# Indexer queries gathered in long runs, sums of squares after one projection, and one broadcast per factor in a two-layer transformer kernel

## The chip, the cores and the metric

The kernel runs on one core of one Trainium2 chip, in one launch. The metric is the device time of the whole launch in microseconds (us); a time "before" is the median of several executions on the chip.

## The reference, cut to what matters

Two identical layers work on 512 tokens of width 1024. Each layer projects the tokens with one matrix, runs two kinds of attention on the pieces (eight heads of latent attention, eight heads of sparse attention), mixes them, and applies a mixture of 16 experts. What the change touches is this:

```python
proj = h @ w_in
qa, kva, kr, dq, dk, dv, iq, ik, iw = split(proj)      # iq: 8 heads x 32
# latent attention
q    = rms_norm(qa, q_norm_g) @ w_q_up                  # qa: 384 wide
c_kv = rms_norm(kva, kv_norm_g)                         # kva: 256 wide
v    = c_kv @ w_uv
# sparse attention: an indexer chooses 128 keys per token
rel   = relu(einsum('bthd,bsd->bths', iq, ik) * 32 ** -0.5)
score = einsum('bths,bth->bts', rel, iw * 8 ** -0.5)
sel   = top_k(where(key <= token, score, -inf), 128)
...
def rms_norm(x, g):
    return x * rsqrt(mean(x * x) + 1e-6) * g
```

## The kernel before, in words

The function `attention(l, ...)` builds one layer's attention. All 512 tokens lie along the free axis of a tile, and the projection is made in 13 column tiles of 128 (`proj(ct)`, L242 to L272). Each column tile is 24 matmuls of 128x128 by 128x512 (L271): the weights are split into a high and a low half (`split`, L163 and L164), and high by high, low by high and high by low are added. The high half is a cast on ScalarE (ACT, L163). The low half is a subtraction of 128x1024 elements (L164), on VectorE (DVE) or GpSimd (POOL); from the fourth column tile on it is on GpSimd. The column tiles come in this order: one small one, two with the indexer's queries (iq), the one with the sparse keys and values (dkv), two with kva, three with qa, four with dq.

**Indexer.** The queries of a column tile are written to memory (`iqd`, L301) and read back by four DMAs (L304), eight a layer, so that one head's 32 rows lie beside one another on 32 partitions. Then, for three blocks of query tokens (i = 1, 2, 3, with 256, 384 and 512 keys) and eight heads each, TensorE makes the scores (L347), ScalarE applies the relu (L352), and VectorE adds the weighted heads (L355 for the first head, L358 for the other seven). The top 128 follow in 16 rounds of a maximum and a replacement on VectorE (MAX, L365, and MATCH_REPLACE, L366), then a comparison (L368) and the distance mask (L372). These rounds are filler: they carry a lower priority, and the scheduler puts them where VectorE has nothing more urgent.

**Norms.** ScalarE squares kva (L336) and qa into `sqk`, `sqq` and `sq2`; GpSimd adds the two squares of kva (L381). TensorE sums over the partitions with matmuls against a column of ones (L418, 4 for kva and 12 for qa in a layer); VectorE divides by the width (`ms`, L422); GpSimd raises to the power -0.5 (`rmsy`, L185) and writes each factor onto a diagonal (`dg`, L427, one instruction of 512 columns for the kva factor and one for the qa factor). A matmul of a matrix of ones with the diagonal (L434) gives every partition the factor of each token: the broadcast. VectorE multiplies kva by it (`kvg`, L439), GpSimd makes the low half of the product (L164, `big<-kvg`), and the value products (L220, L221, L223) and the query products with their scaling (L530) come after.

**Order.** The kernel is built with a scheduler. It places each instruction on its engine's list by priority (the order in which the code is written, lowered for the filler) and by its own estimate of when the inputs are ready; `tc.issue_after(x)` adds the condition that an instruction stands behind x. Each engine then runs its list in order and waits where an input isn't there. So a change in one place can turn the list in another. Hardware queues: all loads and the iq transfers are issued from SyncE.

Of the kernel before, what the change touches and what calls it, by code (L numbers as in the profile page):

```python
# [17 lines left out]
L, T, D = 2, 512, 1024  # L18
NT = T // 128
# [76 lines left out]
def block_kernel(ctx, tc, xT0, x0, win, wqk, wuv, wo, gvec, lnp, rw, rb, wgu, wdn, consts, angles, stripd, rowsd, out):  # L96
    nc = tc.nc
# [19 lines left out]
    def C(name, a=0, b=None):  # L117
        o, w = _C[name]
        return cn[:, o + a:o + (w if b is None else b)]
# [33 lines left out]
    def ps(tag):  # L153
        return psp.tile([128, 512], F32, name=tag, bufs={"mm": 4, "tr": 2, "pv": 2}[tag])

    def bigt(dt=F32):
        return big.tile([128, 2048], dt, name="big")
# [55 lines left out]
    iqd = drm.tile([2, 2, 128, 384], F32, name="iqd")  # L213
# [17 lines left out]
    def attention(l, xh, xl, wraw, first, rest, x_dram):  # L231
# [5 lines left out]
                    load_win(l, i, wraw)  # L237
            return wraw[s]

        done = {}  # L240

        def proj(ct):  # L242
            if l and ct == 0:
# [23 lines left out]
        def project(p, w, ts, jj=(0, 1, 2), end=2):  # L267
            for j in jj:
                for k in range(8):
                    x = (xl if j == 2 else xh)[k // 4][:, k % 4, ts]  # L270
                    nc.tensor.matmul(p[:, ts], w[j == 1][:, k * 128:(k + 1) * 128], x, start=(j + k == 0),  # L271
                                     stop=(j == end and k == 7))  # L272

        ke, ko = x4p("ke")
        at = u4("at")
# [10 lines left out]
        p = proj(T_S)  # L286
# [8 lines left out]
        iq = [bigt(F32R)[:, :1536].rearrange("p (h t) -> p h t", h=4) for _ in range(2)]  # L295
        for i in range(2):
            p = proj(T_IQ + i)
            iqp = u4("iqp", F32R)
            split(iqp[:, :512], iqp[:, 512:], p)

            nc.sync.dma_start(iqd[i].rearrange("j p t -> p j t"),  # L301
                              iqp.bitcast(F32).rearrange("p (j t) -> p j t", j=2)[:, :, 128:])
            for j in range(4):
                nc.sync.dma_start(iq[i][32 * j:32 * (j + 1)].bitcast(F32),  # L304
                                  iqd[i][j // 2].rearrange("(h r) t -> r h t", h=4))
        p = proj(T_DKV)
        dkv, sq2 = u4p("dkv")
        nc.scalar.copy(dkv, p)
# [5 lines left out]
        p = ps("mm")  # L314
# [6 lines left out]
        p = transpose4(dkv, 0)  # L321
        nc.scalar.copy(dvt, p.rearrange("p (a b) -> p a b", a=NT)[:, :, 64:128])
        p = transpose4(S, 0)
# [7 lines left out]
        sqk = u4p("sqk")  # L331
# [7 lines left out]
        for i in range(1, NT):  # L339
# [3 lines left out]
            for h in range(8):  # L343
                if (i, h) in KVA_AT:
                    latents(KVA_AT.index((i, h)))
                p = ps("mm")
                nc.tensor.matmul(p[:, :n], iq[h // 4][:, h % 4, (i - 1) * 128:i * 128], ik4[:, :n],  # L347
                                 start=True, stop=True)
                if h % 4 == 0:
                    rel = bigt()  # L350
                r = rel[:, h % 4 * 512:(h % 4 + 1) * 512]
# [18 lines left out]
            for dd in DD[i]:  # L370
                w = dd.shape[1]
# [27 lines left out]

        dqs = [bigt(F32R).rearrange("p (a b) -> p a b", a=4) for _ in range(2)]  # L400
        vs = bigt().rearrange("p (a b) -> p a b", a=4)
        for i in range(4):
            p = proj(T_DQ + i)
            qh, ql = u4p("dq", F32R)
            nc.scalar.activation(qh, p, AF.Copy, scale=-0.125)
            nc.vector.scalar_tensor_tensor(ql, p, -0.125, qh.bitcast(F32), op0=OP.mult, op1=OP.subtract)
            for s in range(2):
                d = dqs[i // 2][:, i % 2 * 2 + s, :]
                for j, q in enumerate((qh, ql)):
                    b = 64 * (s ^ j)  # L410
                    copy_rows(d[b:b + 64], q[64 * s:64 * (s + 1)])
            if i == 1:

                p = ps("pv")
                for j, qq in enumerate((sqk[:1], sqq)):
                    for t in range(NT):
                        for q in qq:
                            nc.tensor.matmul(p[:, j * 4 + t:j * 4 + t + 1], q[:, t * 128:(t + 1) * 128],  # L418
                                             C("ones", 0, 1), start=(q is qq[0]), stop=(q is qq[-1]))
                ms = sm.tile([128, 8], F32, name="ms")  # L420
                for j, n in enumerate((256, 384)):
                    nc.vector.tensor_scalar(ms[:, 4 * j:4 * j + 4], p[:, 4 * j:4 * j + 4], 1.0 / n, 1e-6,  # L422
                                            op0=OP.mult, op1=OP.add)
                rs, _ = rsqrt(ms, 8, "rms")
                dgt = u4("dg")
                for j in range(2):
                    nc.gpsimd.tensor_tensor(dgt[:, j * 512:(j + 1) * 512].rearrange("p (t a) -> p t a", t=NT),  # L427
                                            ident[:, None, :].to_broadcast([128, NT, 128]),
                                            rs[:, 4 * j:4 * j + 4][:, :, None].to_broadcast([128, NT, 128]), op=OP.mult)
            if i == 2:  # L430
                bc = []
                for j in range(2):
                    p = ps("pv")
                    nc.tensor.matmul(p, C("ones"), dgt[:, j * 512:(j + 1) * 512], start=True, stop=True)  # L434
                    bc.append(p)
        ckt = bigt(F32R)
        ckv = [(ckt[:, 1024 * i:1024 * i + 512], ckt[:, 1024 * i + 512:1024 * (i + 1)]) for i in range(2)]
        for i in range(2):
# [998 lines left out]
def layouts(a):  # L1437
# [4 lines left out]
    qa, kva, kr, dq, dk, dv, iq, ik, iw = np.split(w, np.cumsum([384, 256, 32, 512, 64, 64, 256, 32]), axis=2)  # L1442
    sw = np.concatenate([kr[:, :, 16:], kr[:, :, :16]], axis=2)
    pad = np.zeros((L, D, 24), w.dtype)
    cols = np.concatenate([ik, iw, pad, kr, sw, iq, dk, dv, kva, qa, dq], axis=2)
    win = c(cols.reshape(L, 8, 128, N_COLT, 128).transpose(0, 2, 3, 1, 4)).reshape(L, 128, N_COLT * 1024)
    q = a["w_q_up"].reshape(L, 384, 8, 96)
# [46 lines left out]
```

## Time and profile before

| | |
|---|---|
| median of 3 runs | 1209.43 us (1207.76 to 1210.98) |
| the profiled execution's own time | 1213.77 us |
| its span in the profile | 1212.0 us |
| TensorE matmuls (PE) busy | 1150.3 us, 95% of the span |
| VectorE (DVE) busy | 1026.7 us, 85% |
| ScalarE (ACT) busy | 802.6 us, 66% |
| GpSimd (POOL) busy | 303.4 us, 25% |
| mean granted TensorE clock | 0.98 |

The profile is one execution. Its own time is 4.34 us above the median of the runs and 1.77 us above its span. Shares of busy time are means over very different stages: in the experts TensorE is nearly always busy, while in the attention stage, at 40 to 138 us in the first layer and about 640 to 740 us in the second, VectorE is the busy one. A timeline row gives start, duration, engine, line, operation, output<-inputs and shapes; a bracket gives the idle time before it and what ended it. A row "x2" holds two such instructions in a row.

### The profile page before, as it was taken

What the parts mean: (1) busy time and instruction counts of PE and PEld (TensorE: products, weight loads), DVE (VectorE), ACT (ScalarE), POOL (GpSimd) and SP (SyncE); (2) the same over time, 40 slices, a digit from 0 to 9 for tenths busy, and PEclk for the clock granted to TensorE, in tenths of its full rate; (3) what the DMA queues carried; (4) which work ended last, traced back from release to release, by engine and by line L of the source; (5) the groups of instructions that cost most, each with busy time, mean ns of one, the idle gap of its engine ahead of it and who ended that gap; (6) DMA issues with size and microseconds to landing.
All of it is one profiled execution on the core that took longest, in us unless ns stands there. A gap on an engine that the chain in (4) does not pass through costs nothing. (4 is left out here: it accounts for less than half of the span.)

```text
span 1212.0 us, 16822 instructions
## 1 busy us (share of the span) xinstructions
PE 1150.3 (95%) x5729; PEld 901.6 (74%) x5729; DVE 1026.7 (85%) x1857; ACT 802.6 (66%) x1264; POOL 303.4 (25%) x241
## 2 busy tenths in 40 slices
PE   9999899999999999999898998999999999999995
PEld 6686556778788888887686765567777888888783
DVE  4599977389999999988867999674899999999987
ACT  4533578335788888887544346683358888888872
POOL 2336332121211111200542453322211111111004
PEclk8999999999999999999898999999999999999998
DMA  7626104456999999988235270143669999999841
GB/s 253 200 67 218 51 12 141 161 208 252 391 392 396 388 384 369 383 317 299 84 137 143 70 253 1 51 141 144 234 269 379 400 390 387 394 373 368 304 170 69
DMA packets 56972, 292.20 MB, mean 241 GB/s; under 512 B 10064, under 2 KB 13904, under 8 KB 28465
## 3 DMA queue, kind: packets, MB, share of 16 engines
q1 hardware_dynamic: 47376, 270.48, 60.2%
q0 software_dynamic: 8064, 15.36, 3.5%
q10 hardware_dynamic: 1440, 5.24, 1.1%
q8 instruction: 46, 0.75, 0.2%
q14 instruction: 46, 0.37, 0.1%
HBM read 267.96 MB, written 31.98 MB: 247 GB/s over the span
## 5 line engine op out<-in xcount | busy, mean ns | idle before, releaser
L163 ACT CAST hl<-big 128x1024 fp32r<-128x1024 f32 x438 | 457.1, 1054 | 132.1 <-PE mm L635 46.2
L164 DVE TENSOR_TENSOR hl<-big,hl 128x1024 fp32r<-128x1024 f32 x403 | 483.5, 1226 | 49.7 <-ACT hl L163 42.9
L1056 PE MATMUL mm<-hl,xh 128*128 128x512 f32 x504 | 206.7, 410 | 0.0
L1057 PE MATMUL mm<-hl,xh 128*128 128x512 f32 x504 | 197.4, 392 | 0.0
L1078 PE MATMUL pv<-hl,hT 128*128 128x512 f32 x720 | 172.0, 394 | 0.8 <-DVE hl L164 0.8
L1078 PEld LDWEIGHTS pv<-hl,hT 128*128 128x128 f32 x720 | 136.4, 190 | 30.0 <-DVE hl L164 1.7
L271 PE MATMUL mm<-big,hl 128*128 128x512 f32 (+1 forms) x624 | 141.9, 387 | 1.9 <-ACT hl L163 1.0
L271 PEld LDWEIGHTS mm<-big,hl 128*128 128x128 f32 x624 | 114.3, 195 | 26.8 <-ACT hl L163 2.5
L1020 POOL DMA_INDIRECT xg<-xdr,ii x30 | 53.7, 1790 | 265.0 <-DVE ii L1034 238.9
L164 POOL TENSOR_TENSOR hl<-big,hl 128x1024 fp32r<-128x1024 f32 x35 | 85.9, 2458 | 134.1 <-ACT hl L163 118.8
L1056 PEld LDWEIGHTS mm<-hl,xh 128*128 128x128 f32 x504 | 94.8, 188 | 16.2 <-ACT hl L163 0.3
L1057 PEld LDWEIGHTS mm<-hl,xh 128*128 128x128 f32 x504 | 95.1, 189 | 15.7
L1056 PE MATMUL mm<-hl,xl 128*128 128x512 f32 x252 | 98.8, 392 | 0.0
L1057 PE MATMUL mm<-hl,xl 128*128 128x512 f32 x252 | 98.6, 391 | 0.0
L635 PE MATMUL mm<-hl,big 128*128 128x512 f32 x384 | 95.1, 401 | 0.0
L492 ACT ACTIVATE P<-P,mn 128x128 f32<-128x128 f32 (+3 forms) x128 | 71.9, 568 | 18.6 <-DVE mn L490 16.5
L635 PEld LDWEIGHTS mm<-hl,big 128*128 128x128 f32 x384 | 71.9, 191 | 14.1
L504 ACT COPY big<-tr 128x512 f32<-128x512 f32 (+3 forms) x128 | 49.7, 431 | 36.4 <-PE tr L502 35.5
L502 PE MATMUL tr<-cn,P 128*128 128x128 f32 x320 | 61.8, 293 | 9.8 <-DVE P L498 9.3
L502 PEld LDWEIGHTS tr<-cn,P 128*128 128x128 f32 x320 | 36.0, 141 | 42.8 <-ACT big L504 17.0
L1098 POOL DMA_INDIRECT ydr<-y,ii x26 | 28.2, 1085 | 151.4 <-ACT y L1094 114.1
L572 POOL TENSOR_TENSOR mh<-dd,cn 128x256 f32<-128x256 f32 (+2 forms) x64 | 44.6, 717 | 66.0 <-DVE mn L490 39.8
(279 smaller groups left out, 1861.1 us busy)
## 6 DMA issues: line engine op xcount, KB each, us to landing
big<-wgu SPq DMA_DIRECT2D x128, 1024.0 KB, 8.6
big<-wdn SPq DMA_DIRECT2D x64, 1024.0 KB, 8.2
big<-win SPq DMA_DIRECT2D x10, 1024.0 KB, 5.6
ydr<-zz SPq DMA_DIRECT2D x2, 4096.0 KB
big<-wo SPq DMA_DIRECT2D x8, 1024.0 KB, 14.0
big<-ydr SPq DMA_DIRECT2D x8, 1024.0 KB, 5.3
big<-wqk SPq DMA_DIRECT2D x4, 1024.0 KB, 4.8
big<-dq SPq DMA_DIRECT2D x32, 128.0 KB, 2.3
```

Source lines behind the costliest of these rows:

```text
L163: i = nc.scalar.copy(hi, src).ins
L164: last_lo[0] = (eng or nc.vector).tensor_sub(lo, src, hi.bitcast(F32)).ins
L271: nc.tensor.matmul(p[:, ts], w[j == 1][:, k * 128:(k + 1) * 128], x, start=(j + k == 0), stop=(j == end and k == 7))
L492: nc.scalar.activation(e, e, AF.Exp, bias=mn[:, i:i + 1], scale=-1.0, accum_out=su[:, i:i + 1])
L502: nc.tensor.transpose(p[:, (i - kb) * 128:(i - kb + 1) * 128], P[:, PO[i] + kb * 128:PO[i] + (kb + 1) * 128], ident)
L504: copies.append(nc.scalar.copy(pt[kb], p[:, :512 - 128 * kb]).ins)
L572: last_mask[0] = nc.gpsimd.tensor_tensor(m[:, c:c + w], dd, C("slope", h, h + 1).to_broadcast([128, w]), op=OP.mult)
L635: R["pe"] = nc.tensor.matmul(pp[t][i], x, w[:, i * 512:(i + 1) * 512], start=first, stop=last).ins
L1020: return nc.gpsimd.indirect_dma_start(out=st[e]["xg"], out_offset=None, in_=xdr[l], in_offset=bass.IndirectOffsetOnAxis(ap=st[e]["ii"][:, ...
L1056: nc.tensor.matmul(pg, x, w[:, :512], start=(k == 0 and x is a and w is wh), stop=last)
L1057: nc.tensor.matmul(pu, x, w[:, 512:], start=(k == 0 and x is a and w is wh), stop=last)
L1078: nc.tensor.matmul(py[i], x, w[:, i * 512:(i + 1) * 512], start=(k == 0 and x is a and w is wh), stop=last)
```

## The change

1. On the host, the columns of iq are put in the order (row, head) in place of (head, row), and the DMA of L304 reads 32 runs of 4 heads x 384 tokens instead of 32 times 4 runs of 384 tokens (6144 bytes in a piece where it was 1536). The number of DMAs and their bytes are the same.
2. The four sums for kva, so far free to run as soon as their input was there, are held behind the last matmul of the second dq projection with `issue_after`, together with the twelve for qa.
3. The two broadcasts, so far both behind the third dq projection in the code, are now written one behind the third (kva's) and one behind the fourth (qa's).

```diff
@@ proj, project @@
-        done = {}
+        done, last_mm = {}, [None]
...
-                    nc.tensor.matmul(p[:, ts], w[j == 1][:, k * 128:(k + 1) * 128], x, start=(j + k == 0),
-                                     stop=(j == end and k == 7))
+                    last_mm[0] = nc.tensor.matmul(p[:, ts], w[j == 1][:, k * 128:(k + 1) * 128], x,
+                                                  start=(j + k == 0), stop=(j == end and k == 7)).ins
@@ the queries' way back from memory @@
                 nc.sync.dma_start(iq[i][32 * j:32 * (j + 1)].bitcast(F32),
-                                  iqd[i][j // 2].rearrange("(h r) t -> r h t", h=4))
+                                  iqd[i][j // 2].rearrange("(r h) t -> r h t", h=4))
@@ dq projections, i in 0..3 @@
+        bc = []
...
             if i == 1:
                 p = ps("pv")
-                for j, qq in enumerate((sqk[:1], sqq)):
-                    for t in range(NT):
-                        for q in qq:
-                            nc.tensor.matmul(p[:, j * 4 + t:j * 4 + t + 1], q[:, t * 128:(t + 1) * 128],
-                                             C("ones", 0, 1), start=(q is qq[0]), stop=(q is qq[-1]))
+                with tc.issue_after(last_mm[0]):
+                    for j, qq in enumerate((sqk[:1], sqq)):
+                        for t in range(NT):
+                            for q in qq:
+                                nc.tensor.matmul(p[:, j * 4 + t:j * 4 + t + 1], q[:, t * 128:(t + 1) * 128],
+                                                 C("ones", 0, 1), start=(q is qq[0]), stop=(q is qq[-1]))
...
-            if i == 2:
-                bc = []
-                for j in range(2):
-                    p = ps("pv")
-                    nc.tensor.matmul(p, C("ones"), dgt[:, j * 512:(j + 1) * 512], start=True, stop=True)
-                    bc.append(p)
+            if i >= 2:
+                bc.append(ps("pv"))
+                nc.tensor.matmul(bc[-1], C("ones"), dgt[:, (i - 2) * 512:(i - 1) * 512], start=True, stop=True)
@@ host @@
+    iq = iq.reshape(L, D, 2, 4, 32).transpose(0, 1, 2, 4, 3).reshape(L, D, 256)
     cols = np.concatenate([ik, iw, pad, kr, sw, iq, dk, dv, kva, qa, dq], axis=2)
```

The scheduler turns these edits into new lists; both layers change alike. Line numbers of the changed kernel differ by one or two (L418 is L420, L422 is L424, L427 is L429, L439 is L438). On TensorE, from the sums to the value products (L220), the end of the list before is this:

```order
L418 MATMUL pv<-cn,dkv 128x1
L271 MATMUL mm<-big,hl 128x512 x24
L434 MATMUL pv<-dg,cn 128x512 x2
L271 MATMUL mm<-big,hl 128x512 x24
L220 MATMUL mm<-hl,big 128x512
```

and in the changed kernel:

```order
L420 MATMUL pv<-cn,dkv 128x1
L271 MATMUL mm<-big,hl 128x512 x30
L434 MATMUL pv<-dg,cn 128x512
L271 MATMUL mm<-big,hl 128x512 x18
L434 MATMUL pv<-dg,cn 128x512
L220 MATMUL mm<-hl,big 128x512
```

The first broadcast stands six matmuls into the fourth dq projection, the second at its end. The four kva sums, before behind the fifth of the third block's eight scores (L347), now stand right ahead of the twelve qa sums, after 120 matmuls of five projections.

GpSimd's list around the diagonals, before:

```order
L381 TENSOR_TENSOR sqk<-sqk 128x512
L164 TENSOR_TENSOR hl<-big,hl 128x1024 x4
L164 TENSOR_TENSOR hl<-wv,hl 128x1024
L185 TENSOR_TENSOR rmsy<-ms,mhalf 128x8
L427 TENSOR_TENSOR dg<-cn,rmsy 128x512 x2
L164 TENSOR_TENSOR hl<-big,hl 128x1024 x2
L164 TENSOR_TENSOR big<-kvg,big 128x512 x2
L448 MEMSET zz 128x1024
```

and in the changed kernel:

```order
L381 TENSOR_TENSOR sqk<-sqk 128x512
L164 TENSOR_TENSOR hl<-big,hl 128x1024 x4
L185 TENSOR_TENSOR rmsy<-ms,mhalf 128x8
L164 TENSOR_TENSOR hl<-wv,hl 128x1024
L164 TENSOR_TENSOR hl<-big,hl 128x1024
L429 TENSOR_TENSOR dg<-cn,rmsy 128x512 x2
L164 TENSOR_TENSOR hl<-big,hl 128x1024
L164 TENSOR_TENSOR big<-kvg,big 128x512 x2
```

Two low halves, of `wv` and of a dq weight, now stand between the power (`rmsy`) and the diagonals. VectorE's list around the kva product, as a difference (minus is before, plus is the change; the numbered tiles are the rounds' maxima):

```order
 L365 MAX m_520<-aw 128x8
-L406 SCALAR_TENSOR_TENSOR dq<-mm,dq 128x512
-L439 TENSOR_TENSOR kvg<-kvg,pv 128x512 x2
 L366 MATCH_REPLACE aw<-m_520,aw 128x384
+L407 SCALAR_TENSOR_TENSOR dq<-mm,dq 128x512
+L438 TENSOR_TENSOR kvg<-kvg,pv 128x512 x2
 L365 MAX m_523<-aw 128x8
```

The product stands one replacement later. Past this, the lists of the softmax stages of both layers also differ in many places, by a few instructions each.

## Rows read from the trace of the kernel before

**Rows 1.** Waits of VectorE, 40 to 138 us: output line <- releaser: us, times, longest

```profile
DVE aw L355 <- ACT big L352: 7.3, 1, 7.3
DVE big L164 <- ACT big L163: 1.4, 1, 1.4
```

**Rows 2.** Timeline of TensorE, second layer, indexer

```profile
640.73 0.73 PE L347 MATMUL mm<-ik,big 128*128 128x256 f32 x4 [0.92 <-DMA big<-iqd]
644.66 4.12 PE L347 MATMUL mm<-ik,big 128*128 128x256 f32 x12 [3.21 <-DMA big<-iqd]
648.58 6.68 PE L271 MATMUL mm<-big,hl 128*128 128x512 f32 x24
...
657.88 1.05 PE L418 MATMUL pv<-cn,sqk 128*128 128x1 f32 x8 [0.37 <-POOL sqk L381]
```

**Rows 3.** Windows: length, busy PE, PEld, DVE, ACT, POOL, PEclk, DMA share, GB/s

```profile
636.00:644.00 8.00, 4.53 (x21) 3.37 (x19) 1.73 (x1) 3.48 (x8) 4.36 (x2) 1.00 1.08 216
644.00:651.00 7.00, 6.34 (x18) 5.23 (x19) 6.09 (x15) 4.33 (x12) 0.37 (x1) 0.52 0.30 116
645.00:646.00 1.00, 1.00 (x5) 0.88 (x5) 0.79 (x3) 0.76 (x3) 0.00 (x0) 0.50 0.93 385
```

**Rows 4.** Timeline of GpSimd and VectorE, second layer, start of the first block

```profile
642.03 2.34 POOL L164 TENSOR_TENSOR hl<-big,hl 128x1024 fp32r<-128x1024 f32 x1 [3.29 <-ACT hl L163]
...
642.27 2.38 DVE L355 SCALAR_TENSOR_TENSOR aw<-big,iwt,at 128x256 f32<-128x256 f32 x1 [7.78 <-ACT big L352]
```

**Rows 5.** Timeline of ScalarE and GpSimd, second layer, the third weight half of this stretch

```profile
665.22 0.69 ACT L387 ACTIVATE qg<-mm,gv 128x512 fp32r<-128x512 f32 x1 [3.41 <-PE mm L271]
...
666.93 2.57 POOL L164 TENSOR_TENSOR hl<-big,hl 128x1024 fp32r<-128x1024 f32 x1 [2.59 <-ACT hl L163]
...
672.37 2.85 POOL L164 TENSOR_TENSOR hl<-big,hl 128x1024 fp32r<-128x1024 f32 x1 [2.87 <-ACT hl L163]
```

**Rows 6.** Timeline of VectorE, second layer, end of the first block

```profile
664.56 0.43 DVE L368 TENSOR_TENSOR aw<-aw 128x256 f32<-128x256 f32 x1
...
667.16 2.89 DVE L358 SCALAR_TENSOR_TENSOR aw<-big,iwt,aw 128x512 f32<-128x512 f32 x1
```

**Rows 7.** VectorE by line and shape, 60 to 80 us: count, busy us, mean ns, idle

```profile
L358 DVE SCALAR_TENSOR_TENSOR aw<-big,iwt,aw 128x512 f32<-128x512 f32 x7 | 9.5, 1353 | 0.0
```

**Rows 8.** Timeline of GpSimd, first layer, around the diagonals

```profile
92.18 1.66 POOL L185 TENSOR_TENSOR rmsy<-ms,mhalf 128x8 f32<-128x8 f32 x1 [5.94 <-DVE ms L422]
93.92 2.04 POOL L427 TENSOR_TENSOR dg<-cn,rmsy 128x512 f32<-128x512 f32 x2
95.91 4.74 POOL L164 TENSOR_TENSOR hl<-big,hl 128x1024 fp32r<-128x1024 f32 x2
100.61 2.55 POOL L164 TENSOR_TENSOR big<-kvg,big 128x512 fp32r<-128x512 f32 x2
```

**Rows 9.** Timeline of TensorE, first layer, from the sums to the query products

```profile
88.07 5.75 PE L271 MATMUL mm<-big,hl 128*128 128x512 f32 x24
95.01 2.12 PE L434 MATMUL pv<-dg,cn 128*128 128x512 f32 x4 [1.19 <-POOL dg L427]
...
102.44 0.39 PE L220 MATMUL mm<-hl,big 128*128 128x512 f32 x1
...
107.89 0.39 PE L220 MATMUL mm<-qg,hl 128*128 128x512 f32 x1
```

**Rows 10.** Timeline of VectorE, first layer, around the kva product

```profile
99.20 1.27 DVE L439 TENSOR_TENSOR kvg<-kvg,pv 128x512 f32<-128x512 f32 x2
100.39 0.08 DVE L366 MATCH_VALUE_LOAD aw<-m,aw 128x8 f32 x1
100.47 0.54 DVE L366 MATCH_REPLACE8 aw<-m,aw 128x384 f32<-128x384 f32 x1
...
103.29 0.55 DVE L368 TENSOR_TENSOR aw<-aw 128x384 f32<-128x384 f32 x1
...
113.46 0.68 DVE L530 TENSOR_TENSOR q<-mm,ct 128x512 f32<-128x512 f32 x1
```

## The prediction

> **What bounds the kernel now.** I first read the waits of each engine, then the timelines of the two attention stages, because the change touches only these. VectorE waits 7.3 us for its first indexer addition in the first layer, once 1.4 us for a cast, and then not again until 138 us [rows 1]; the second layer reads alike, with 7.78 us ahead of its first addition [rows 4]. From the first addition to the softmax stage VectorE therefore has an unbroken list, with the top-k rounds as filler, and sets the end of the stretch. TensorE runs ahead of it. Its waits in that stretch, 0.92 and 3.21 us for the queries in the second layer [rows 2] and 1.19 us for the first diagonal [rows 9], are waits of an engine that isn't the bound: a microsecond taken from them reaches the end only where it lets VectorE's list run faster.
>
> One thing does make VectorE's list longer: a GpSimd subtraction that runs beside it. At 667.16 an addition L358 takes 2.89 us and ends with the GpSimd half that began at 666.93 [rows 5, 6]. In the first layer seven additions of that shape took 9.5 us with a mean of 1.353 us [rows 7]: two held at 2.89 and five at (9.5 - 5.78) / 5 = 0.74 us, so a hold costs 2.15 us. The additions, L368 and L372 read two tiles and are open to it; the rounds (MAX, MATCH_REPLACE) run at their usual length beside such a subtraction, as at 100.47 beside the one that began at 95.91 and ended at 100.65 [rows 8, 10].
>
> **Part 1, the gather.** While the eight gathers run, the DMA engines are fully busy (share 1.08) at 216 GB/s; in a window with a plain weight load they move 385 GB/s at a share of 0.93 [rows 3]. The time of a gather is thus not bytes alone, and runs four times as long should bring it near the second figure. Eight times 192 KB (1.57 MB) take 7.3 us at 216 and 4.1 us at 385 GB/s: 3.2 us less. The bounds are 0 (the rate stays) and 3.2. I take 3.2, as the destination of the weight load is also long rows. The Trainium skill says otherwise: its page "DMA: Bandwidth & Descriptors", section Specifications, gives 512 bytes as the least transfer for full rate, which the old 1536 bytes meet; by it this term would be 0. The trace speaks against that reading, with busy engines at 216 GB/s, but no run here yet shows longer runs of this gather. It is the third rival below.
>
> In the second layer the two waits for queries (4.13 us) shrink to 0.9 us. With them goes a low clock: the granted clock is 0.52 in 644 to 651 us and 0.50, the lower of its two levels (1.2 GHz), within that [rows 3], right behind the wait of 3.21, and the 24 matmuls at 648.58 took 6.68 us instead of 5.75 [rows 2, 9], 0.93 us. In the first layer the queries are in time, and nothing goes.
>
> VectorE's first addition in the second layer starts at 642.27 and is held to 644.65 by a GpSimd half [rows 4]. That half depends on weights and not on queries, so VectorE's start stays.
>
> **Part 2, the sums.** Four kva sums and their wait (1.05 and 0.37 us [rows 2]) leave the third block's scores; about 0.9 us of it comes back behind the second dq projection. TensorE is some 1.4 us further ahead in between, in both layers.
>
> **What the lead does.** GpSimd's halves follow ScalarE's casts, and these stand behind products that wait for TensorE (L387 waited 3.41 us for it [rows 5]). So the halves at 666.93 and 672.37 come earlier by the lead: 3.2 + 0.9 + 1.4 = 5.5 us in the second layer with all terms, 3.2 with the gather alone; I take 4.4. The first then runs from 662.5 to 664.9, beside rounds, which aren't held, and only clips L368 at 664.56 [rows 6] by 0.4 us. The second, at 668, still holds one addition. Gain: 2.15 - 0.4 = **1.75 us**, in the second layer. Bounds: 0 (lead under 2 us) and 2.15. In the first layer the halves lie alike, but the lead is 1.4 us, at most 2.4 if a low clock behind the sums goes too: both halves stay in VectorE's open stretch, gain **0**, bounds 0 and 0.7.
>
> **Part 3, the broadcasts.** This is where the new lists cost. The power ends at 92.18 + 1.66 = 93.84. Before, the diagonals came at once (2.04 for two, 1.02 each) and TensorE waited 1.19 us [rows 8, 9]. Now two halves of 4.74 / 2 = 2.37 us stand between: 93.84 + 4.74 = 98.6, first diagonal at 99.6. The power itself doesn't move, since VectorE's ms stands behind as much work as before. TensorE arrives at about 94.9: the sums end near 87.7 and 30 matmuls of 5.75 / 24 = 0.24 us take 7.2. So it waits **about 4.7 us** in place of 1.2, in each layer. The broadcast takes 2.12 / 2 = 1.06, so kva's factor is there at 100.7. VectorE, which took the product at 99.20, has one more replacement ahead of it (0.54 + 0.08 [rows 10]) and comes at 99.8: a new wait of **0.9 us** on the bounding engine, per layer. Queued behind it are the rest of the rounds, L368 and L372, so all of it counts. Bounds: 0 (the halves get done before the power, as the wv half did in the old list) and 2.4 (one more half in front).
>
> Then GpSimd's kva halves (2.55 for two [rows 8]) can start only at about 103.1, as VectorE's product ends at 102 and a weight half ends at 103.1. They then run beside L368 (103.29 before, 104.2 now [rows 10]) and L372; each can be held by up to 1.3 us less its own 0.55. Bounds 0 and 1.4; I take **0.7**, the middle, as the rows don't tell which comes first.
>
> TensorE's lateness isn't passed on further: behind the first broadcast 18 matmuls (4.3), a broadcast (1.06), the value products (107.89 - 102.44 = 5.45 [rows 9]) and the first query product (9 matmuls, 2.0) end at 99.6 + 1.1 + 4.3 + 1.1 + 5.45 + 2.0 = 113.6. VectorE takes its first query product (113.46 [rows 10]) at 113.46 + 1.6 - 0.68 = 114.4, as it now stands one replacement earlier. Slack: 0.8 us.
>
> **Softmax stages.** They are reordered by a few instructions. I cost this at nothing, because the work is the same and VectorE is busy; if that cover is gone, one more held instruction costs 2.15 us per layer, and the single wait of 1.4 us [rows 1] is what could be gained.
>
> **Sum.** First layer 0 + 0.9 + 0.7 = +1.6; second -1.75 + 0.9 + 0.7 = -0.15; together **+1.45 us** on the profiled execution's 1213.77, whose time is 4.34 above the median of the runs. On the median: 1209.43 + 1.45 = 1210.9. A measurement of this kernel can tell about 0.3%, 3.6 us, from no change: 1205.8 to 1213.1.
>
> **Rivals.**
> (a) TensorE is the bound after all: it is busy nearly throughout, and its removed waits come off the end: 4.1 + 0.9 + 0.7 (twice 0.37) + 2.4 (twice 1.19) = 8.1 us, 1201.3. Against it: VectorE's empty list of waits. Chance 0.14.
> (b) Slower: the new wait of 4.7 us on TensorE brings the low clock that followed the wait of 3.21 us [rows 2, 3]. There the clock was 0.52 for 7 us, which costs 3.4 us; less the slack of 0.8 the query products come 2.6 us late for VectorE, in each layer: 1210.9 + 5.2 = 1216. It decides once the clock is low for over 1.6 us behind the first broadcast. For it: the wait is longer than 3.21. Against it: the first broadcast's old waits of about 1.2 brought none, and TensorE was busy just before. Chance 0.18.
> (c) The gather gets no faster, because its 216 GB/s [rows 3] has another cause than the length of its runs. Then the second layer's lead is 1.4 us, the hold at 666.93 stays, and the sum is +3.2: 1212.6. This is the rival that the change doesn't do what it says. For it: eight gathers beside one another, each to a quarter of the partitions, differ from the weight load in more than run length. Chance 0.13. The rule of the Trainium skill's page "DMA: Bandwidth & Descriptors" (Specifications) cited above speaks for it too.
>
> **How the numbers follow.** My forecast has 0.55: 0.43 within 0.3%, and 0.06 on either side for the softmax stages. (a) is faster, 0.14. (b) is slower, 0.18. (c) gives 0.09 within and 0.04 beyond. So faster 0.20, same 0.52, slower 0.28. The range is 1205.5 to 1216.5: downward one hold of 2.15 us less in each layer than forecast, and 1.1 us for the new VectorE waits not coming; upward (b). It leaves out (a) and the ends of the others.
>
> **What would show it.** Right: the queries' waits in the second layer gone or under 1 us; one L358 of 2.9 us instead of two there, two still in the first layer; a wait of TensorE at L434 for dg of 4 to 5 us per layer; a VectorE wait at L438 for pv of about 0.9 us. Wrong: a TensorE wait at L434 under 2 us (the weight halves got out of the way), clock 0.5 behind it (b), gathers still at 216 GB/s (c), or an end that moves by over 4 us while VectorE's attention stretches keep their length (a).

## The result and the profile after

The changed kernel takes 1217.13 us (median of 6 runs, 1213.59 to 1221.9) against 1210.3 us (6 runs, 1207.76 to 1212.12). The ratio is 1.0061 with a 95% interval of 1.0041 to 1.0081: **slower by 0.6%, about 7 us**. The forecast was 1210.9, its range ended at 1216.5, and both were wrong.

One correction to the section on the change: the second GpSimd half that now stands between the power and the diagonals is not of a dq weight but of `wuk`, the weight of the latent keys. Its duration and place are as told there.

**Where the time went.** Four rows cut the attention of each layer at the same work: VectorE's first L355, the first kva product, TensorE's first mixing matmul (L635, now L634). The rows of before that don't stand in [rows 4, 10] are these, from the timelines of VectorE and TensorE:

```profile
42.76 0.48 DVE L355 SCALAR_TENSOR_TENSOR aw<-big,iwt,at 128x256 f32<-128x256 f32 x1 [7.25 <-ACT big L352]
210.70 1.10 PE L635 MATMUL mm<-hl,big 128*128 128x512 f32 x4
...
700.60 1.28 DVE L439 TENSOR_TENSOR kvg<-kvg,pv 128x512 f32<-128x512 f32 x2
813.51 1.09 PE L635 MATMUL mm<-hl,big 128*128 128x512 f32 x4
```

and of the changed kernel:

```profile
43.06 0.48 DVE L355 SCALAR_TENSOR_TENSOR aw<-big,iwt,at 128x256 f32<-128x256 f32 x1 [7.26 <-ACT big L352]
101.46 1.28 DVE L438 TENSOR_TENSOR kvg<-kvg,pv 128x512 f32<-128x512 f32 x2 [1.11 <-PE pv L434]
216.07 1.09 PE L634 MATMUL mm<-hl,big 128*128 128x512 f32 x4
...
644.17 2.38 DVE L355 SCALAR_TENSOR_TENSOR aw<-big,iwt,at 128x256 f32<-128x256 f32 x1 [7.81 <-ACT big L352]
704.30 1.28 DVE L438 TENSOR_TENSOR kvg<-kvg,pv 128x512 f32<-128x512 f32 x2 [0.91 <-PE pv L434]
818.07 1.09 PE L634 MATMUL mm<-hl,big 128*128 128x512 f32 x4
```

Differences of these starts, in us (first addition to product, product to mixing, in each layer):

| | layer 1 | | layer 2 | | sum |
|---|---|---|---|---|---|
| before | 56.44 | 111.50 | 58.33 | 112.91 | 339.18 |
| after | 58.40 | 114.61 | 60.13 | 113.77 | 346.91 |

All four stretches are longer, by 7.73 us together. Outside them the profiled execution of the change is 1.6 us the shorter (spans of 1218.1 and 1212.0 us); the medians differ by 6.8. Ahead of the kva product it is 1.96 + 1.80; 0.62 of each is the replacement that now stands ahead of the product and isn't lost [rows 10]. So 2.5 us are lost there and 5.2 behind it, where the forecast had put 0.7 a layer.

**The diagonals.** GpSimd's timeline in the first layer of the changed kernel answers to [rows 8]:

```profile
92.64 1.66 POOL L185 TENSOR_TENSOR rmsy<-ms,mhalf 128x8 f32<-128x8 f32 x1 [8.50 <-DVE ms L424]
94.28 2.38 POOL L164 TENSOR_TENSOR hl<-wv,hl 128x1024 fp32r<-128x1024 f32 x1
96.63 2.34 POOL L164 TENSOR_TENSOR hl<-big,hl 128x1024 fp32r<-128x1024 f32 x1
98.94 2.03 POOL L429 TENSOR_TENSOR dg<-cn,rmsy 128x512 f32<-128x512 f32 x2
100.93 2.37 POOL L164 TENSOR_TENSOR hl<-big,hl 128x1024 fp32r<-128x1024 f32 x1
103.27 2.53 POOL L164 TENSOR_TENSOR big<-kvg,big 128x512 fp32r<-128x512 f32 x2
```

The power is done at 94.30 (before 93.84), but the diagonals start at 98.94 where they started at 93.92. TensorE's timeline, first and second layer, answers to [rows 9]:

```profile
89.68 6.08 PE L271 MATMUL mm<-big,hl 128*128 128x512 f32 x26
100.02 1.40 PE L434 MATMUL pv<-dg,cn 128*128 128x512 f32 x2 [4.27 <-POOL dg L429]
100.58 6.33 PE L271 MATMUL mm<-big,hl 128*128 128x512 f32 x18
...
692.02 9.93 PE L271 MATMUL mm<-big,hl 128*128 128x512 f32 x30
703.13 1.12 PE L434 MATMUL pv<-dg,cn 128*128 128x512 f32 x2 [1.18 <-POOL dg L429]
703.70 4.69 PE L271 MATMUL mm<-big,hl 128*128 128x512 f32 x18
```

In the first layer TensorE waits 4.27 us, and the 18 matmuls behind the wait take 6.33 us where the same 18 take 4.69 in the second layer. In the second layer the wait is only 1.18, since TensorE was slow before it: 30 matmuls took 9.93 us. The windows over both places show why (length, busy PE, PEld, DVE, ACT, POOL, granted clock, DMA share, GB/s):

```profile
100.90:104.30 3.40, 3.40 (x9) 2.42 (x8) 2.84 (x7) 1.22 (x2) 3.40 (x3) 0.52 0.51 116
691.00:698.20 7.20, 7.20 (x23) 5.87 (x23) 6.92 (x20) 2.96 (x4) 2.51 (x2) 0.53 0.27 84
152.10:158.90 6.80, 6.00 (x17) 4.25 (x17) 6.05 (x22) 3.86 (x13) 4.69 (x10) 0.51 0.02 5
```

The granted clock is at its lower level (0.5, 1.2 GHz) behind the wait in the first layer, from the end of the sums on in the second, and a third time in the softmax stage, behind waits that come below. In the second layer's softmax stage the kernel before has such a fall too (0.50 in 753.20 to 756.60).

**VectorE.** The wait for the broadcast is 1.11 and 0.91 us (the kva products above). GpSimd's two kva halves now run beside L368, which [rows 10] shows at 0.55 us; VectorE's timeline, both layers:

```profile
104.91 1.31 DVE L368 TENSOR_TENSOR aw<-aw 128x384 f32<-128x384 f32 x1
...
707.75 1.61 DVE L368 TENSOR_TENSOR aw<-aw 128x384 f32<-128x384 f32 x1
```

**The softmax stage.** What the forecast had not looked for stands here. VectorE's timeline before, first layer:

```profile
142.80 0.75 DVE L372 SCALAR_TENSOR_TENSOR dd<-aw,at 128x384 f32<-128x384 f32 x2
...
158.27 0.29 DVE L490 CUSTOM_DVE_ANT_0 P<-mm,at 128x128 f32<-128x128 f32 x1 [1.31 <-PE mm L545]
```

and after:

```profile
145.86 0.56 DVE L372 SCALAR_TENSOR_TENSOR dd<-aw,at 128x384 f32<-128x384 f32 x1
...
147.76 2.96 DVE L164 TENSOR_TENSOR hl<-big,hl 128x1024 fp32r<-128x1024 f32 x1
...
151.73 0.61 DVE L372 SCALAR_TENSOR_TENSOR dd<-aw,at 128x128 f32<-128x128 f32 x1
152.85 0.69 DVE L489 CUSTOM_DVE_ANT_0 P<-mm,mh 128x512 f32<-128x512 f32 x1 [0.52 <-POOL mh L571]
...
164.53 0.29 DVE L489 CUSTOM_DVE_ANT_0 P<-mm,at 128x128 f32<-128x128 f32 x1 [4.32 <-PE mm L544]
```

The distance mask of the last block has two pieces, 384 and 128 wide. Before, they ran back to back ("x2"). Now the small one runs 5.9 us behind the other, after a latent head's scores (L489) and a weight half that VectorE makes itself, and the first sparse head waits for the mask that GpSimd makes of the piece (`mh`). Before, the half stood behind the masks, and nothing held it; now a GpSimd half begins 0.47 us ahead of it and holds it (GpSimd of the change, then VectorE of before):

```profile
147.29 2.35 POOL L164 TENSOR_TENSOR hl<-big,hl 128x1024 fp32r<-128x1024 f32 x1
...
153.99 1.22 DVE L164 TENSOR_TENSOR hl<-big,hl 128x1024 fp32r<-128x1024 f32 x1
```

So 1.7 of the 5.9 us are a hold. TensorE, for which VectorE has to empty the scores, waits too, first for the scores that stand behind the held half, then for those that wait for the mask:

```profile
151.25 0.38 PE L557 MATMUL mm<-kk,big 128*128 128x256 f32 x1 [1.90 <-DVE mn L489]
...
153.61 0.80 PE L557 MATMUL mm<-kk,big 128*128 128x512 f32 x1 [0.78 <-DVE mn L489]
```

Its clock is low right behind (the third window above), and VectorE pays with 4.32 us of idle time at 164.53 where it paid 1.31. From the mask to the first mixing matmul, first layer, before and after (columns as above):

```profile
142.80:210.70 67.90, 63.62 (x347) 39.48 (x345) 52.67 (x175) 51.26 (x159) 27.69 (x40) 1.00 0.20 64
145.86:216.07 70.21, 65.52 (x344) 41.78 (x342) 52.28 (x174) 50.66 (x158) 27.18 (x40) 0.95 0.19 62
```

VectorE isn't busy for longer; the stretch is 2.3 us longer at a lower mean clock. In the second layer (744.22 to 813.51, and 748.53 to 818.07) it is 69.29 and 69.54 us, with a clock of 0.98 in both. So of the 7.73 us, 2.6 arise behind this mask, nearly all in the first layer, and 5.2 ahead of it.

**The gather.** A window of the changed kernel over its eight gathers in the second layer, and TensorE's two waits behind them:

```profile
638.00:646.00 8.00, 4.41 (x21) 3.24 (x19) 1.83 (x1) 3.35 (x8) 4.47 (x2) 1.00 1.01 229
```

```profile
642.69 0.71 PE L347 MATMUL mm<-ik,big 128*128 128x256 f32 x4 [0.98 <-DMA big<-iqd]
646.39 3.94 PE L347 MATMUL mm<-ik,big 128*128 128x256 f32 x12 [2.99 <-DMA big<-iqd]
```

The DMA engines are as full as before (share 1.01 against 1.08) and move 229 GB/s instead of 216 [rows 3]. The waits are 0.98 and 2.99, before 0.92 and 3.21 [rows 2]. SyncE waited 2.0 us for the write of the queries (before 0.4), but counted from VectorE's first addition, which is itself 1.90 us later, the queries came when they did before. No lead came of the gather. The halves of [rows 5] start at 667.07 and 672.51; counted from the first addition that is 1.76 us earlier than before, about the 1.4 us forecast for the moved sums alone. That is too little: they still hold two additions, now in the 384-wide block; grouped by line and form, 640 to 690 us:

```profile
L358 DVE SCALAR_TENSOR_TENSOR aw<-big,iwt,aw 128x384 f32<-128x384 f32 x7 | 6.4, 913 | 0.0
L355 DVE SCALAR_TENSOR_TENSOR aw<-big,iwt,at 128x384 f32<-128x384 f32 x1 | 2.8, 2755 | 0.0
```

### The profile page after: what moved, and what is told of

It is laid out like the page before. It is cut to its first block, busy times and chain, and to the rows that moved or that the text cites. A ratio compares the mean times of both kernels' runs of the same rounds, so it can differ in the third digit from the quotient of the medians.

```text
span 1218.1 us, 16828 instructions
## 1 busy us (share of the span) xinstructions
PE 1154.0 (95%) x5729; PEld 906.2 (74%) x5729; DVE 1028.7 (84%) x1857; ACT 802.4 (66%) x1264; POOL 302.2 (25%) x241
## 5 line engine op out<-in xcount | busy, mean ns | idle before, releaser
L271 PE MATMUL mm<-big,hl 128*128 128x512 f32 (+1 forms) x624 | 144.8, 391 | 4.7 <-ACT sqq L389 2.1
L634 PE MATMUL mm<-hl,big 128*128 128x512 f32 x384 | 95.1, 401 | 0.0
L634 PEld LDWEIGHTS mm<-hl,big 128*128 128x128 f32 x384 | 71.9, 191 | 14.1
```

What stands on the lines that cost most here:

```text
L271: last_mm[0] = nc.tensor.matmul(p[:, ts], w[j == 1][:, k * 128:(k + 1) * 128], x, start=(j + k == 0), stop=(j == end and k == 7)).ins
L634: R["pe"] = nc.tensor.matmul(pp[t][i], x, w[:, i * 512:(i + 1) * 512], start=first, stop=last).ins
```

## The experiments

Every kernel was timed in 5 rounds; ratios are to the kernel before on the same chip, with 95% intervals. The first three do one part of the change alone.

**e1_gather: the long runs alone.**

```diff
-                                  iqd[i][j // 2].rearrange("(h r) t -> r h t", h=4))
+                                  iqd[i][j // 2].rearrange("(r h) t -> r h t", h=4))
...
+    iq = iq.reshape(L, D, 2, 4, 32).transpose(0, 1, 2, 4, 3).reshape(L, D, 256)
```

> Only the gather's long runs (host columns and the read pattern). All engine lists stay as before. Theory A (the diagonals stand too late on GpSimd): no difference, 1210.3 within 3.6 us. Theory C (the new softmax order costs by itself): also no difference, since the order is the old one. If the run length did limit the gather, the waits of TensorE for the queries fall from 4.1 to under 1 us in the second layer and one held addition goes (about -2 us); if not, they stay at about 4.

1211.25 against 1211.62 us, 0.999 [0.9975, 1.0005]. Its window at 636 to 644 us shows 219 GB/s at a DMA share of 1.00. The longer runs are worth nothing that can be measured here.

**e2_sums: the sums behind the second dq projection, alone.**

```diff
+                    last_mm[0] = nc.tensor.matmul(p[:, ts], w[j == 1][:, k * 128:(k + 1) * 128], x,
...
-                for j, qq in enumerate((sqk[:1], sqq)):
+                with tc.issue_after(last_mm[0]):
+                    for j, qq in enumerate((sqk[:1], sqq)):
...
```

> Only the sums behind the second dq projection; both broadcasts stay together behind the third. GpSimd's list gets the two halves between power and diagonals, as in the whole change. Theory A: nearly the whole loss, +4 to +7 us, with a wait of TensorE at the first broadcast over 4 us in the first layer. Theory B (the split of the broadcasts is what costs): under +2 us.

1218.16 us, 1.0049 [1.003, 1.0069]. GpSimd's list has the two halves ahead of the diagonals, and VectorE waits 1.8 and 1.3 us for the broadcast. The distance pieces stay together. TensorE's wait was 2.75 us in the first layer, where over 4 was expected, and 4.3 in the second.

**e3_split: one broadcast each behind the third and fourth projection, alone.**

```diff
+        bc = []
...
-            if i == 2:
-                bc = []
-                for j in range(2):
-                    p = ps("pv")
-                    nc.tensor.matmul(p, C("ones"), dgt[:, j * 512:(j + 1) * 512], start=True, stop=True)
-                    bc.append(p)
+            if i >= 2:
+                bc.append(ps("pv"))
+                nc.tensor.matmul(bc[-1], C("ones"), dgt[:, (i - 2) * 512:(i - 1) * 512], start=True, stop=True)
```

> Only the two broadcasts split. GpSimd's list around the diagonals stays as before. Theory A: within 3.6 us of before; the kva product on VectorE starts as before, to 0.7 us. Theory C (any new softmax order costs some 3 us in the first layer): +2 to +4 us, with the product at its old time and the end of the attention late.

1215.44 us, 1.0041 [1.0022, 1.006]. The kva product is on time. What is late is the small distance piece (149.89 us against 142.80 before), and in both layers a GpSimd weight half (103.14, 706.28) holds the second block's mask L372: 2.50 and 2.48 us in place of 0.54. That is a third way, which neither theory had.

So two parts lose, by different ways, and their losses don't add up (0.49 and 0.41%, together 0.61). The next kernels repair the ways one by one.

**e4_diag_first: the whole change, GpSimd's diagonals first.**

```diff
...
-        wvh, wvl = granule(wv, 0, nc.gpsimd)
+        with tc.issue_after(last_dg[0]):
+            wvh, wvl = granule(wv, 0, nc.gpsimd)
...
-        wuk = granule(wqs[0], 0, nc.gpsimd)
+        with tc.issue_after(kv_lo):
+            wuk = granule(wqs[0], 0, nc.gpsimd)
```

> The whole change, but on GpSimd the diagonals come right behind the power, then the wv half, one weight half, the two kva halves, and the wuk half behind these. Theory A: the first wait at the broadcast falls under 1.5 us, VectorE's wait at the kva product goes, and most of the loss with it: 1209 to 1213 us. Theory C: the product is on time, but the softmax stages still end late: 1213 to 1217 us.

1218.37 us, 1.0052 [1.0034, 1.007], above both forecasts: no repair. The scheduler gave the diagonals another buffer, and GpSimd waited 3.10 us, until 97.39, for a replacement of VectorE's (L366) to leave it. The distance piece is late too.

**e5_split_dist: e3, and the last block's distance pieces at normal priority.**

```diff
+            if i == NT - 1:
+                tc.cur_priority = keep
             for dd in DD[i]:
```

> The split of the broadcasts alone (as e3), but the last block's distance masks keep normal priority, so that the 128-wide piece stands right behind the 384-wide one on VectorE as in the list before, and no longer behind a latent head's scores. Theory D (the late distance piece holds the sparse heads' masks, TensorE waits and its clock falls): the time from the kva product to the first mix product is back from about 115.3 and 116.0 us to 111.5 and 113 us in the two layers, and the whole to 1210 to 1213 us. Theory C (any new order costs): stays at 1214 to 1217 us.

1213.54 us, 1.0026 [1.0013, 1.0039]. The pieces stand together again, VectorE's half is behind them as before the change and takes 1.21 us (e3: 2.99), and the hold of L372 stays. In all kernels with the late piece the half is early and held, at 2.96 to 2.99 us; no run separates the two.

**e6_dist: the whole change with the edit of e5.**

> The whole change, with the distance masks early as in e5 and nothing else. Theory D and A together: the kva product stays 2 us late in both layers, but the stretch behind it falls from 114.6 and 113.8 to about 112 and 113 us: 1212 to 1215 us. If the late diagonals were all of it (A alone): 1216 to 1218 us.

1218.15 us, 1.0049 [1.0028, 1.007]. The time fits the second forecast, although in the profiled execution the stretches behind the product fell to 112.90 and 113.45 us as the first one said. That execution took 1214.15, 4 us less than the median, so it doesn't stand for the others.

**e7_pool_order: the whole change with GpSimd's old order** (`wv` half, power, diagonals, then two halves), by an ordering without a wait.

```diff
...
+        tc.add_manual_dep(rs_ins, last_lo[0].name, mybir.DependencyInfo(mybir.DependencyClass.NoSync,
+                                                                        mybir.DependencyReason.DATA), reason="order")
...
-        wuk = granule(wqs[0], 0, nc.gpsimd)
+        with tc.issue_after(last_dg[0]):
+            wuk = granule(wqs[0], 0, nc.gpsimd)
```

> The whole change, with GpSimd's list around the diagonals as before (wv half, power, diagonals, two weight halves), the distance piece still late. A and D together: the kva product comes at its old time to 0.7 us (56.4 and 58.3 us behind the first addition), the softmax stretch stays at 114 to 115 us: 1213 to 1216 us. A alone: 1209 to 1212 us.

1217.85 us, 1.006 [1.0042, 1.0078], above both forecasts. The wait for the broadcast is gone, but a weight half now begins just ahead of L372 in the second layer and holds it for 2.71 us.

**e8_both: the edits of e5 and e7 on the whole change.**

> Both repairs on the whole change: GpSimd's list as before and the distance masks early. A and D together: nothing is left of the loss, 1209 to 1212 us. If a third cause (the new order elsewhere, or the sums in one block and the low clock behind them) counts: over 1213 us.

1217.31 us, 1.0056 [1.004, 1.0072]. The wait for the broadcast is gone and the distance pieces stand together, and yet nothing is gained: in both layers a weight half begins 0.1 us ahead of L372 (here L374). GpSimd and VectorE in the second layer:

```profile
704.58 2.40 POOL L164 TENSOR_TENSOR hl<-big,hl 128x1024 fp32r<-128x1024 f32 x1
...
704.67 2.73 DVE L374 SCALAR_TENSOR_TENSOR dd<-aw,at 128x384 f32<-128x384 f32 x1
```

The first layer reads alike, with 2.72 us for the mask. This profiled execution took 1213.22 us, 4 less than the median; the 10 executions lie between 1211.23 and 1219.61.

To test the hold as a cause, work was added. A second memset of the same zeros (0.95 us) goes into GpSimd's list behind the first, and the next weight half behind it. A memset reads nothing, and the half starts about 1 us later:

```diff
-            nc.gpsimd.memset(zz, 0.0)
+            nc.gpsimd.memset(zz, 0.0); zz2 = nc.gpsimd.memset(zz, 0.0).ins
...
-                wqu.append(granule(wqs[(j // 8 + 1) // 2], (j // 8 + 1) % 2, nc.gpsimd))
+                with (tc.issue_after(zz2) if j // 8 == 1 else ExitStack()): wqu.append(granule(wqs[(j // 8 + 1) // 2], (j // 8 + 1) % 2, nc.gpsimd))
```

**e9_split_dist_pad: e5 with the memset.**

> e5 with one more GpSimd memset of 0.95 us behind the one of zz, so that the next weight half starts 0.95 us later; every engine's list is otherwise that of e5. Theory H (VectorE's distance mask of the second block is held by that half: 2.50 us in place of 0.54 in both layers of e5): the mask escapes, the softmax stretches fall from 114.5 and 115.3 us to 112.5 and 113.3, and the time falls by 3 to 4 us although work was added. If holds don't reach the end (D, or the new order alone): no change, or up to 2 us slower.

1211.88 us, 1.0001 [0.9986, 1.0016], where e5 had 1.0026. The second layer, first of e5 (GpSimd, then VectorE):

```profile
704.84 2.41 POOL L164 TENSOR_TENSOR hl<-big,hl 128x1024 fp32r<-128x1024 f32 x1
...
705.18 2.48 DVE L374 SCALAR_TENSOR_TENSOR dd<-aw,at 128x384 f32<-128x384 f32 x1
```

and of e9:

```profile
704.14 1.97 POOL L448 MEMSET zz<- 128x1024 f32 x2
706.06 2.40 POOL L164 TENSOR_TENSOR hl<-big,hl 128x1024 fp32r<-128x1024 f32 x1
...
705.38 0.54 DVE L374 SCALAR_TENSOR_TENSOR dd<-aw,at 128x384 f32<-128x384 f32 x1
```

In e5 the half begins 0.34 us ahead of the mask (L372, here L374) and the mask ends 0.41 us behind the half's end, as the addition of [rows 5, 6] does with 0.55. In e9 it begins 0.68 us behind the mask, which takes its 0.54 us.

**e10_both_pad: e8 with the memset.**

> e8 with the same added memset. Theory H: the same mask escapes in both layers (2.72 to 0.55 us each), the softmax stretches fall from 115.0 and 114.7 to about 113 and 112.6 us, the whole by 3 to 4 us, to 1213 or 1214. Otherwise: as e8, 1217 us or more.

1210.13 against 1210.25 us, 1.0006 [0.9989, 1.0022]. The added work took 0.5% away, some 6 us where 3 to 4 were expected: the whole change with three repairs costs what the kernel before costs, to some 0.2%. In the two profiles the masks account for 4.4 us; the rest lies behind them, where e8's clock falls once in each layer and e10's doesn't.

**e11_before_pad: the control, the kernel before with the memset.**

> Control: the kernel before with the same added memset. There the mask runs ahead of the half and isn't held, so theory H expects no change from before (within 0.2%); a half that is late for the query products (a cost of the memset itself) would show as a wait of TensorE and up to 1 us per layer.

1210.41 us, 0.9996 [0.998, 1.0012]. In itself the memset neither costs nor gains.

**e12_split_pad: e3 with the memset.**

> e3 (the split alone) with the same added memset, every list otherwise that of e3. Theory H: the mask (2.50 us in e3) escapes in both layers; softmax stretches from 115.3 and 116.0 to about 113.3 and 114.0; the whole 3 to 4 us below e3. What is left over before (some 2 us) is theory D's part, the late distance piece.

1212.27 us, 1.0019 [1.0004, 1.0034], where e3 had 1.0041. What is left is the late distance piece.

The last three complete the table for the whole change, since its own profile shows no held L372 in the second block.

**e13_pad: the change with the memset. e14_dist_pad: also the edit of e5. e15_order_pad: the memset and the edit of e7.**

> The whole change with the extra memset of 0.95 us in GpSimd's list and nothing else repaired; the other engines' lists stay those of the change. Theory (three pieces: kva's diagonals late, the last distance piece late, a hold by a GpSimd half): the change's own profile showed no hold of the second block's L372, so the memset should take away 0 to 2 us: 1215 to 1217, and TensorE's wait for the first diagonal of 4 us in the first layer stays. Rival (the place of GpSimd's halves alone carries the loss): 1210 to 1211.

> The whole change with the early distance masks and the memset, the diagonals left late. Theory (three pieces): the late diagonals are what is left, 1 us for the late product and up to 1.5 us for the low clock behind TensorE's wait in each layer: 1213 to 1215, VectorE's wait for the kva broadcast of about 1 us in each layer, idle time of the softmax stage as before the change. Rival (the diagonals' delay is absorbed; hold and distance carry it): within 1 us of the kernel before, 1209.5 to 1211.

> The whole change with GpSimd's order of before around the diagonals and the memset, the distance piece left late. Theory (three pieces): as the split with the memset, which lost 2.0 us, since only the late distance piece is left: 1211.5 to 1213. Rival (the distance piece costs nothing once no half is in the way): 1209.5 to 1211.

1218.03, 1215.93 and 1214.31 us against 1210.39: each above the range that the theory gave, by 1.0, 0.9 and 1.3 us. The rivals, which put them near 1210 or 1211, fall. The theory's mechanisms stand, and its sizes were too small. All ratios of the whole change:

| | nothing repaired | distance early | old GpSimd order | both |
|---|---|---|---|---|
| without the memset | 1.0061 [1.0041, 1.0081] | 1.0049 [1.0028, 1.007] | 1.006 [1.0042, 1.0078] | 1.0056 [1.004, 1.0072] |
| with the memset | 1.0065 [1.0046, 1.0084] | 1.0046 [1.003, 1.0063] | 1.0032 [1.002, 1.0044] | 1.0006 [0.9989, 1.0022] |

Read the lower row: there no weight half holds the second block's mask. The late diagonals cost 0.33% (1.0065 less 1.0032) or 0.40% (1.0046 less 1.0006), 4.0 to 4.8 us; the late distance piece 0.19% or 0.26%, 2.3 to 3.1 us. The second is within what the intervals leave open (they overlap), but e3 against e5 (0.15%) and e12 against e9 (0.18%) have the same sign. The upper row differs from the lower only where the old GpSimd order is restored: there the hold and what follows it cost 0.28 and 0.50%. The traces give the same sizes: the four stretches above add up to 346.84 us in e13, 344.21 in e14, 342.21 in e15 and 339.44 in e10, against 339.18 before. The waits of VectorE for its scores in the softmax stage of the first layer bear the second cause out; e15 (distance late), then e10 (early), both with the old GpSimd order:

```profile
DVE P L493 <- PE mm L548: 8.2, 7, 3.7
```

```profile
DVE P L495 <- PE mm L550: 6.2, 7, 2.2
```

## Why the prediction was wrong

**Part 1, the gather (no gain; forecast 3.2 us earlier queries).** The step that failed is "The time of a gather is thus not bytes alone, and runs four times as long should bring it near the second figure." Fully busy engines at a low rate were read as the cost of short runs, against a weight load that differs in more than run length. The third rival held, and e1 shows it alone. The Trainium skill's rule in "DMA: Bandwidth & Descriptors", Specifications (512 bytes are enough for full rate) agrees with the trace: 6144-byte runs moved 229 GB/s in the changed kernel and 219 in e1, against 216 with 1536-byte ones, and no time was gained. Why the gather fills the engines at some 220 GB/s no run shows.

**The lead (forecast -1.75 us in the second layer).** It hung on part 1 and fell with it: 1.76 us of lead are left, inside the "under 2 us" for which the forecast itself gave no gain, and the two holds are still there. Without this term the sum was +3.2.

**Part 3, the diagonals.** The step itself was right: VectorE's new wait is 1.11 and 0.91 us for 0.9, TensorE's 4.27 for 4.7 in the first layer, L368 is held by 1.31 - 0.55 = 0.76 and 1.61 - 0.55 = 1.06 us for 0.7, which was to cover L372 as well; that one wasn't held. In the second layer TensorE's wait was 1.18 because the clock was low ahead of it, which the forecast did not have; VectorE's wait came out the same, since the diagonals' own time sets it. The credit was misplaced: the two halves came between with the move of the sums (e2 has them, e3 hasn't), not with the split. The term was mis-sized: 1.6 a layer, 3.2 us in all, against 4.0 to 4.8 measured. Counted from its first addition, VectorE comes to the last block's mask 2.76 and 2.41 us later than before, with the same instructions behind it: 2.02 us are the waits for the broadcast, 1.82 the holds of L368, 0.35 a wait that the next point explains, and 1.0 are spread over small differences.

**The second rival: its condition came true, its price didn't.** In the first layer the clock fell behind the 4.27 us wait, and 18 matmuls lost 6.33 - 4.69 = 1.64 us. But the query products didn't come late for VectorE: its first one starts at 115.53, 2.07 later than in [rows 10], and stands behind a round without a wait. All that VectorE waits for behind the kva product, until the softmax stage, is 0.35 us at 107.63, for a copy of the last dq projection. In the second layer no fall follows the broadcast. So the rival's 1216, one us from the measured time, is luck.

**The softmax stages (forecast 0).** The failed step is "I cost this at nothing, because the work is the same and VectorE is busy". The work is the same, but one 128-wide piece of about 0.2 us (0.75 for two, 0.56 for the wide one) has a consumer on GpSimd, and through it TensorE has one. It slid 5.9 us behind its neighbour, and VectorE's half came ahead of it and was held, for 2.3 to 3.1 us in the two layers together. The split alone does that (e3, and not e2). The loss goes by the clock: from this mask to the mixing the profiles show 67.9 us at a mean clock of 1.00 or 69.2 to 69.3 at 0.98 with the order of before (before, e10, e11, e14), and 69.5 at 0.98 or 70.2 at 0.95 with the late piece (after, e13, e15). At the same clock the late piece costs 0.3 us; it costs more where the clock falls for longer, and how often it does over many executions was not measured. The bound given, 2.15 us a layer for a held instruction, covered the size but was left out of the sum. With the memset the two measured terms add up to 0.59%, 7.1 us, whichever is repaired first, and the kernel lost about 7; without it both repairs together gain next to nothing (1.0061 to 1.0056), since the hold takes their place.

**Why the repairs failed at first.** The forecast looked for holds of additions by weight halves and of L368 and L372 by kva halves, not of L372 by a weight half. The split and the restored GpSimd order each move GpSimd's list against VectorE's by 0.5 to 0.75 us there (e8, e5), and such a hold of 2 us comes of it. The kernel before runs clear of it by little, as VectorE and GpSimd in its second layer show:

```profile
705.76 0.54 DVE L372 SCALAR_TENSOR_TENSOR dd<-aw,at 128x384 f32<-128x384 f32 x1
...
706.17 2.41 POOL L164 TENSOR_TENSOR hl<-big,hl 128x1024 fp32r<-128x1024 f32 x1 [0.59 <-ACT hl L163]
```

A half 0.41 us earlier would have held the mask. The Trainium skill states the rule in "SBUF — State Buffer", Who interferes with whom: the two engines share one pair of ports, an exclusive lock, and a VectorE instruction with two SBUF inputs contends with a GpSimd instruction that reads SBUF, not with one that only writes it. The trace agrees: the mask takes 2.48 us beside a half that began ahead of it, and 0.54 where only the memset runs.

One reading of the prediction is put right by this: the held addition L358 doesn't end with the half (669.50) but 0.55 us behind it. No term hung on that.

Left open: what the late piece costs without the early half, and how often the clock falls in executions that weren't profiled; and whether any order of these lists beats the kernel before. None of the 15 did by more than its interval.

## What to carry to other kernels

When an edit only reorders, price it by the lists that come out: for each instruction that slid back, find its consumer's consumer, however small the instruction is. Where two engines exclude each other at a port, the distance between two starts decides over a multiple of an instruction's time, so a repair should be judged together with what it slides into, and a pad of idle work is a cheap way to tell a hold from a real delay. A busy queue at a low rate does not say that its descriptors are short; test that alone before building on it.

## What the runs showed of the hardware

**Added work can shorten a kernel.** Some 0.95 us of GpSimd memset a layer took e8 from 1.0056 to 1.0006 and left the kernel before where it was (0.9996).

**The low clock also comes ahead of and behind places that no edit touched.** In the mixing stage of the kernel before the same work took 75.3 us in the first layer and 73.7 in the second, by the windows from its first matmul to the first of the experts:

```profile
210.70:286.00 75.30, 71.97 (x413) 59.69 (x412) 48.56 (x116) 29.47 (x47) 13.59 (x8) 0.98 0.50 188
813.50:887.20 73.70, 70.38 (x414) 58.57 (x412) 48.54 (x116) 29.51 (x47) 13.58 (x8) 1.00 0.52 193
```

In the first, the clock was at 0.50 from 258.2 to 261.6 us, behind a wait of TensorE of 2.32 us for VectorE (L912); the second has the same wait of 2.32 us and no fall. In the changed kernel the fall stands in the second layer. So a single profiled execution carries some 1.6 us for each such fall, and the attention stages have them too, as the softmax stage showed. That is why totals are taken from the medians.
